# Moving the stored sums of weight blocks from VectorE to GpSimd, with 12 instead of 14 seven-product pairs per half and six load buffers in even turns

## The chip, the core and the metric

The kernel is written in Bass with the Tile scheduler and runs on one core of a Trainium2 chip. The metric is the device time of one launch in microseconds (us), the median of the runs shown. TensorE (PE) multiplies, VectorE (DVE) and ScalarE (ACT) do elementwise work, GpSimd (POOL) does elementwise work and issues DMAs from its own queue, and SyncE (SP) issues most DMAs.

## The reference

One layer of a hybrid block over 256 rows of 2048 channels, in float32:

```python
h = _rmsnorm(x, attn_norm);  proj = h @ w_in            # 2048 x 13,896
# three branches: stick-breaking attention, top-k sparse attention, memory cross-attention
merged = (gates[:, :, 0] * (o_sb @ w_branch[0]) + gates[:, :, 1] * (o_dsa @ w_branch[1])
          + gates[:, :, 2] * (o_mem @ w_branch[2]))
x = x + merged @ w_out
h2 = _rmsnorm(x, ffn_norm)
u = _causal_dwconv(h2 @ w_up, conv_w, conv_b)           # 2048 x 11,008
g, val = jnp.split(u, 2, axis=-1)
return x + (jax.nn.silu(g) * val) @ w_down              # 5504 x 2048
```

Nearly all of the work is streaming weights once through TensorE: 256 rows are two blocks of 128, and every weight is used for both.

## The kernel before, in words

**Weight tiles.** `weight_tiles` lists all weights in the order of use, as tiles of 128 x 1024 float32 (512 KB). For each, `w_tiles` (L165) loads it on SP's queue into one of four `raw` buffers, ACT rounds it to `whi` (L172), DVE subtracts to get the remainder `wlo` (L173), and PE multiplies hi by hi, lo by hi and hi by lo (L104, three matmuls for one product). `whi` and `wlo` have three buffers each. L172 and L173 are issued at high priority: the scheduler, which fixes each engine's order before the run, may put them ahead of work written earlier.

**Stages.** Keys and values of the memory and the projections (weight tiles 1 to 107); then three merges of 48 tiles each, with 48 tiles of stick-breaking projections after the first; then 32 tiles of `w_out`; then 172 tiles of `w_up` with the convolution; then `w_down` in two halves of 1024 columns. In a merge (L577) each of four column chunks takes 8 gate tiles into the PSUM tile `pg`, then DVE adds the bias (L588, `th`), ACT takes tanh (L589), 4 branch tiles go into `pb`, and DVE multiplies and adds (L596, L597, `acc`). In the merge that `turn_merged` follows, PE transposes `acc` (L810) and ACT and DVE split it into `mg` (L205, L209). The stick-breaking projections end each 4-tile chunk with ACT L757 and DVE L758 (`skT`, `sqT`).

**Pairs in w_down.** The 43 blocks of 128 rows of `w_down` go in pairs. A plain pair takes two tiles and 8 block products (24 matmuls, 12 for each tile). A seven-product pair (`Half.seven`, L983) uses sums of blocks instead: 7 products (21 matmuls), but four loads: half a tile, one tile, and two tiles of stored sums. `SEVEN` (L44) lists which pairs of 0 to 21 are made so. The first two loads go to `raw`, the stored sums to `w_t`, two buffers in the pool `dn` (L993).

**Stored sums.** The sums of weight blocks are made earlier in the same launch, as side work: a generator `weight_sums` (L282) that `step` advances once per weight tile. Each unit (a pair and a half) has two 512 KB loads on GpSimd's queue (L290), four DVE subtractions of 128 x 512 (L293) and two 512 KB stores (L312). Two buffers of 1 MB alternate. 17 units run in steps of 8 tiles from the first merge on, 11 more in steps of 6 from the last merge on. The subtractions are issued under `keep_in_program_order`, and so is each L173 while side work is under way, in w_tiles:

```python
low = nc.vector.tensor_sub(lo[:, :kn * n], raw[:, :kn * n], hi[:, :kn * n].bitcast(F32))
if side:
    tc.keep_in_program_order(low)
```

Instructions so marked keep the order in which they are written among themselves.

## Time and profile before

| What | Value |
|---|---|
| Median of 3 runs | 1878.86 us (1871.59 to 1879.55) |
| Profiled execution: its own time / its span | 1879.46 us / 1877.7 us |
| Granted TensorE clock, mean | 0.98 |
| PE / DVE / ACT / POOL busy, share of the span | 92% / 64% / 49% / 4% |
| HBM read / written | 380.85 MB / 35.91 MB |
| Chain that ended last, by engine | PE 53%, DMA 5%, DVE 5%, ACT 4%, issue 3% |

The shares are averages over stages. A view by stretches of time shows how busy each engine was in each stage, the granted clock, and what the DMA engines moved; the view of waits says which instruction an idle engine waited for. [...]

### The profile page before, as it was taken

What the parts mean: (1) busy time and instruction counts of PE and PEld (TensorE: products, weight loads), DVE (VectorE), ACT (ScalarE), POOL (GpSimd) and SP (SyncE); (2) the same over time, 40 slices, a digit from 0 to 9 for tenths busy, and PEclk for the clock granted to TensorE, in tenths of its full rate; (3) what the DMA queues carried; (4) which work ended last, traced back from release to release, by engine and by line L of the source; (5) the groups of instructions that cost most, each with busy time, mean ns of one, the idle gap of its engine ahead of it and who ended that gap; (6) DMA issues with size and microseconds to landing.
All of it is one profiled execution on the core that took longest, in us unless ns stands there. A gap on an engine that the chain in (4) does not pass through costs nothing.

```text
span 1877.7 us, 22959 instructions
## 1 busy us (share of the span) xinstructions
PE 1736.8 (92%) x8334; PEld 1434.0 (76%) x8334; DVE 1208.3 (64%) x1839; ACT 913.9 (49%) x1217; POOL 72.9 (4%) x182
## 2 busy tenths in 40 slices
PE   8999999999878998888888899999999999898988
PEld 6888889777767777676666678888888888566666
DVE  6696665876445556445555557787877787556656
ACT  6555544344336355333333345555555555445453
POOL 0000000000000100000100000000000000000000
PEclk9999999999999999899999999999999999999999
DMA  8855456577665767666777765555556666878885
GB/s 310 281 188 171 155 168 217 179 252 280 231 213 189 262 234 252 207 201 233 252 242 243 267 206 187 188 190 190 190 190 208 199 207 199 283 252 278 274 264 178
DMA packets 123969, 418.28 MB, mean 223 GB/s; under 512 B 13904, under 2 KB 18896, under 8 KB 123856
## 3 DMA queue, kind: packets, MB, share of 16 engines
q1 hardware_dynamic: 106192, 352.84, 56.3%
q0 software_dynamic: 17088, 63.45, 9.4%
q8 instruction: 65, 1.06, 0.2%
q10 hardware_dynamic: 576, 0.53, 0.1%
q14 instruction: 48, 0.39, 0.1%
HBM read 380.85 MB, written 35.91 MB: 222 GB/s over the span
## 4 chain that ended last, share of the span: by engine, by line
PE 53%; DMA 5%; DVE 5%; ACT 4%; issue 3%; DVEq 0%; SPq 0%; ACTq 0%; POOL 0%; POOLq 0%
PE pj L104 47%; DMA w_t<-sums 5%; PE pj L973 4%; DVE wlo L999 2%; ACT whi L998 2%; DVE wlo L173 2%; ACT whi L172 1%; PE s L973 1%; DVE th L596 0%; DMA w_sums<-in_wts 0%; PE s L104 0%; DVE acc L597 0%; ACT L790 0%; DMA sx<-sx 0%; DMA sums<-w_sums 0%
## 5 line engine op out<-in xcount | busy, mean ns | idle before, releaser
L172 ACT ACTIVATE whi<-raw 128x1024 fp32r<-128x1024 f32 (+2 forms) x503 | 531.5, 1057 | 768.4 <-PE pj L104 606.4
L173 DVE TENSOR_TENSOR wlo<-raw,whi 128x1024 fp32r<-128x1024 f32 (+2 forms) x503 | 609.8, 1220 | 280.8 <-ACT whi L172 279.8
L104 PE MATMUL pj<-whi,xc 128*128 128x512 f32 (+2 forms) x1536 | 480.5, 391 | 1.5 <-ACT whi L172 1.0
L104 PE MATMUL pj<-x2c,whi 128*128 128x512 f32 x1376 | 477.5, 391 | 0.0
L104 PE MATMUL pj<-x2c,wlo 128*128 128x256 f32 x1376 | 386.3, 281 | 0.0
L104 PEld LDWEIGHTS pj<-whi,xc 128*128 128x128 f32 x1536 | 290.9, 192 | 58.5 <-ACT whi L172 1.4
L104 PE MATMUL pj<-wlo,xc 128*128 128x512 f32 (+2 forms) x768 | 301.3, 392 | 28.9 <-DVE wlo L173 28.9
L104 PEld LDWEIGHTS pj<-x2c,whi 128*128 128x128 f32 x1376 | 257.5, 187 | 55.8
L104 PEld LDWEIGHTS pj<-x2c,wlo 128*128 128x128 f32 x1376 | 260.7, 189 | 0.0
L104 PEld LDWEIGHTS pj<-wlo,xc 128*128 128x128 f32 x768 | 147.3, 192 | 62.8 <-DVE wlo L173 35.3
L973 PE MATMUL pj<-whi,fc 128*128 128x512 f32 (+1 forms) x420 | 140.9, 392 | 4.9 <-ACT whi L998 4.4
L999 DVE TENSOR_TENSOR wlo<-w_t,whi 128x1024 fp32r<-128x1024 f32 x56 | 68.0, 1225 | 66.7 <-ACT whi L998 66.5
L973 PEld LDWEIGHTS pj<-whi,fc 128*128 128x128 f32 x420 | 79.6, 191 | 24.3 <-ACT whi L998 7.7
L973 PE MATMUL pj<-wlo,fc 128*128 128x512 f32 (+1 forms) x210 | 85.1, 405 | 13.6 <-DVE wlo L999 11.4
L998 ACT ACTIVATE whi<-w_t 128x1024 fp32r<-128x1024 f32 x56 | 58.5, 1057 | 77.5 <-DMA w_t<-sums 43.0
L104 PE MATMUL pj<-xc,whi 128*128 128x512 f32 x256 | 95.9, 414 | 0.0
L104 PE MATMUL pj<-xc,wlo 128*128 128x256 f32 x256 | 76.1, 297 | 15.2 <-DVE wlo L173 15.2
L104 PE MATMUL pj<-whi,mc 128*128 128x512 f32 x256 | 83.4, 404 | 6.9 <-ACT whi L172 6.9
L104 PE MATMUL pj<-whi,mg 128*128 128x512 f32 x256 | 83.9, 406 | 0.0
L293 DVE TENSOR_TENSOR w_sums<-w_sums 128x512 f32<-128x512 f32 x112 | 76.8, 686 | 4.5 <-DMA w_sums<-in_wts 4.4
L999 DVE TENSOR_TENSOR wlo<-raw,whi 128x512 fp32r<-128x512 f32 (+1 forms) x56 | 52.5, 955 | 28.2 <-ACT whi L998 28.2
L104 PE MATMUL pj<-wlo,mg 128*128 128x512 f32 x128 | 52.6, 411 | 13.3 <-DVE wlo L173 13.3
(261 smaller groups left out, 1930.4 us busy)
## 6 DMA issues: line engine op xcount, KB each, us to landing
raw<-in_wts SPq DMA_DIRECT2D x553, 512.0 KB, 4.2
w_sums<-in_wts POOLq DMA_DIRECT2D x56, 512.0 KB, 5.1
sums<-w_sums POOLq DMA_DIRECT2D x56, 512.0 KB, 6.0
w_t<-sums SPq DMA_DIRECT2D x56, 512.0 KB, 4.5
raw<-in_wts SPq DMA_DIRECT2D x30, 256.0 KB, 4.4
th<-in_bg SPq DMA_DIRECT2D x24, 256.0 KB, 5.8
raw<-in_wts SPq DMA_DIRECT2D x5, 492.0 KB, 3.2
sx<-sx_out POOLq DMA_DIRECT2D x6, 384.0 KB, 4.6
```

Of the source, the lines that this page charges most:

```text
L104: nc.tensor.matmul(o, l, r, start=start, stop=stop, skip_group_check=True)
L172: nc.scalar.activation(hi[:, :kn * n], raw[:, :kn * n], AF.Copy)
L173: low = nc.vector.tensor_sub(lo[:, :kn * n], raw[:, :kn * n], hi[:, :kn * n].bitcast(F32))
L293: tc.keep_in_program_order(nc.vector.tensor_sub(d, x_, y_))
L973: keep(nc.tensor.matmul(o, l[a], r[b], start=first and i == 0, stop=stop and i == 2, skip_group_check=True))
L998: keep(nc.scalar.activation(hi, raw, AF.Copy))
L999: keep(nc.vector.tensor_sub(lo, raw, hi.bitcast(F32)))
```

## The change

- The four subtractions of a unit are issued to GpSimd instead of DVE, between the unit's loads and stores in the same queue, all kept in program order. There is one buffer instead of two. A unit begins with a copy of one column of the newest `wlo` tile to a small tile `pace`, on GpSimd. `L173` (L182 in the changed file) is no longer kept in program order.
- `SEVEN` has 12 pairs instead of 14, 24 units in all (16, then 8), each in steps of 8 tiles. The pairs now come in twos with a plain pair between them.
- In the last stage, loads of either kind of pair take `raw`, `raw` and `raw_more` in turn (four and two buffers); `w_t` is gone. The residual is loaded at block 9 instead of 13.

```diff
-SEVEN = (2, 3, 4, 5, 7, 8, 9, 10, 12, 13, 14, 16, 17, 18)
-UNITS = 17
+SEVEN = (2, 3, 5, 6, 8, 9, 11, 12, 14, 15, 17, 18)
+UNITS = 16
...
+    def buffer():
+        turns[0] += 1
+        if more and turns[0] % 3 == 0:
+            return more[0].tile([P, 1024], F32, name="raw_more", bufs=2)
+        return wraw.tile([P, 1024], F32, name="raw")
...
-        raw = wraw.tile([P, 1024], F32, name="raw")
+        raw = buffer()
...
-                low = nc.vector.tensor_sub(lo[:, :kn * n], raw[:, :kn * n], hi[:, :kn * n].bitcast(F32))
-                if side:
-                    tc.keep_in_program_order(low)
+                nc.vector.tensor_sub(lo[:, :kn * n], raw[:, :kn * n], hi[:, :kn * n].bitcast(F32))
+            now[0] = lo
...
     def weight_sums(w, units, every):
...
-            for i in range(2):
-                nc.gpsimd.dma_start(w[n % 2][:, i], wts[down_at[2 * p + i, c0]])
-        def sub(d, x_, y_):
-            tc.keep_in_program_order(nc.vector.tensor_sub(d, x_, y_))
...
+        a, b = w[:, 0], w[:, 1]
+        for c0, p in units:
+            tc.keep_in_program_order(nc.gpsimd.tensor_copy(pace, now[0][:, 0:1].bitcast(F32)))
+            for i in range(2):
+                tc.keep_in_program_order(nc.gpsimd.dma_start(w[:, i], wts[down_at[2 * p + i, c0]]))
+            for d, x_, y_ in ((a[:, h0], a[:, h1], a[:, h0]), (a[:, h1], a[:, h1], b[:, h1]),
+                              (b[:, h1], b[:, h1], a[:, h0]), (b[:, h0], b[:, h0], b[:, h1])):
+                tc.keep_in_program_order(nc.gpsimd.tensor_sub(d, x_, y_))
             for i in range(2):
-                nc.gpsimd.dma_start(sums_d[c0, p][i], w[n % 2][:, i])
-            for _ in range(every - 5):
+                tc.keep_in_program_order(nc.gpsimd.dma_start(sums_d[c0, p][i], w[:, i]))
+            for _ in range(every):
                 yield
...
-        side.append(weight_sums([h8("w_sums").rearrange("p (i c) -> p i c", c=1024) for i in range(2)], units[UNITS:], 6))
+        side.append(weight_sums(h8("w_sums").rearrange("p (i c) -> p i c", c=1024), units[UNITS:], 8))
...
-                    raw = wraw.tile([P, 1024], F32, name="raw") if j < 2 else dn.tile([P, 1024], F32, name="w_t", bufs=2)
-                    raw = raw[:, :n]
+                    raw = buffer()[:, :n]
...
-                    if before is not None and k == 13:
+                    if before is not None and k == 9:
                         e = residual(c0)
```

How the instructions then stand on their engines is shown at three places.

DVE, the last merge, one column chunk, before (`th<-pj,th` waits for the last of the 8 gate tiles, `th<-th,pj` for the last of the 4 branch tiles):

```order
L293 TENSOR_TENSOR w_sums<-w_sums 128x512
L588 TENSOR_TENSOR th<-pj,th 128x1024
L173 TENSOR_TENSOR wlo<-raw,whi 128x1024
L293 TENSOR_TENSOR w_sums<-w_sums 128x512
L173 TENSOR_TENSOR wlo<-raw,whi 128x1024 x3
L293 TENSOR_TENSOR w_sums<-w_sums 128x512
L596 SCALAR_TENSOR_TENSOR th<-th,pj 128x512 x2
L597 TENSOR_TENSOR acc<-acc,th 128x512 x2
L173 TENSOR_TENSOR wlo<-raw,whi 128x1024
```

and in the changed kernel:

```order
L182 TENSOR_TENSOR wlo<-raw,whi 128x1024 x7
L581 TENSOR_TENSOR th<-pj,th 128x1024
L182 TENSOR_TENSOR wlo<-raw,whi 128x1024 x4
L589 SCALAR_TENSOR_TENSOR th<-th,pj 128x512 x2
L182 TENSOR_TENSOR wlo<-raw,whi 128x1024
L590 TENSOR_TENSOR acc<-acc,th 128x512 x2
L182 TENSOR_TENSOR wlo<-raw,whi 128x1024 x7
```

Counted from the start of the program, 115 `wlo` subtractions stand ahead of the first `th<-pj,th` before, and 117 in the changed kernel; the gate tile it waits for is the 115th tile. At each of the 24 waits of this kind in the three merges the count is the number of the tile waited for before, and two more now.

POOL, the first units, in the changed kernel (before, the same queue held only the loads and stores):

```order
L298 COPY pace<-wlo 128x1
L300 DMA w_sums<-in_wts 128x1024 x2
L303 TENSOR_TENSOR w_sums<-w_sums 128x512 x4
L305 DMA sums_2_98<-w_sums 128x1024 x2
L298 COPY pace<-wlo 128x1
```

The next unit's copy now stands behind the whole unit before it.

SP, the first loads after the residual `e` at the start of the last stage, before:

```order
L930 DMA e_12924<-x2d_96 128x1024 x2
L995 DMA w_t_13005<-sums_0_2_97 128x1024
L995 DMA w_t_13011<-sums_0_2_97 128x1024
L995 DMA raw_13038<-in_wts 128x512
L995 DMA raw_13044<-in_wts 128x1024
L995 DMA raw_13083<-in_wts 128x512
L995 DMA w_t_13050<-sums_0_3_98 128x1024
L995 DMA w_t_13056<-sums_0_3_98 128x1024
```

and in the changed kernel:

```order
L924 DMA e_12891<-x2d_97 128x1024 x2
L171 DMA raw_more_12942<-in_wts 128x1024
L988 DMA raw_more_12972<-sums_0_2_98 128x1024
L988 DMA raw_13005<-in_wts 128x512
L988 DMA raw_more_13011<-in_wts 128x1024
L988 DMA raw_13017<-sums_0_3_99 128x1024
L988 DMA raw_13023<-sums_0_3_99 128x1024
```

The load of a plain tile (block 3) now stands behind `e`, and loads follow in the order of use.

## The prediction

> **What bounds the kernel now.** I first read the busy time by stretches, cut where the stages change. Columns: the stretch, its length, then PE, PEld, DVE, ACT and POOL busy (count), granted clock, DMA share, GB/s.

> ```profile
> 0.00:100.00 100.00, 92.62 (x395) 75.10 (x396) 63.45 (x145) 59.25 (x95) 1.88 (x12) 1.00 0.84 289
> 100.00:314.00 214.00, 213.46 (x1054) 181.28 (x1053) 153.85 (x383) 109.85 (x206) 0.62 (x2) 1.00 0.53 172
> 314.00:1131.00 817.00, 720.60 (x3224) 586.00 (x3222) 449.05 (x606) 338.35 (x418) 59.80 (x115) 0.96 0.68 233
> 1131.00:1599.00 468.00, 468.00 (x2703) 413.17 (x2702) 372.35 (x536) 272.43 (x354) 7.46 (x47) 1.00 0.59 194
> 1599.00:1878.00 279.00, 242.08 (x968) 178.49 (x966) 169.65 (x173) 134.03 (x146) 3.18 (x6) 0.97 0.77 256
> ```

> PE is full in the second and fourth stretch: the projections and w_up are bound by TensorE, and the change touches neither. PE idles 96.4 us (817 - 720.6) in the third, where the side work runs, and 36.9 us in the last. What PE waited for in the third stretch (total, times, longest), then the longest in the last:

> ```profile
> PE pj L104 <- DVE wlo L173: 74.6, 39, 4.2
> PE s L104 <- ACT pT L790: 8.2, 4, 2.6
> PE t L810 <- DVE acc L597: 7.0, 4, 1.8
> ...
> PE pj L973 <- DVE wlo L999: 11.4, 18, 0.8
> ```

> So DVE delivers `wlo` late in the third stretch, though it is busy for only 449 of 817 us. The timeline around one such wait, PE and then DVE:

> ```profile
> 901.81 0.39 PE L104 MATMUL pj<-whi,osb 128*128 128x512 f32 x1
> 904.42 0.50 PE L104 MATMUL pj<-wlo,osb 128*128 128x512 f32 x1 [2.22 <-DVE wlo L173]
> ...
> 902.01 1.23 DVE L588 TENSOR_TENSOR th<-pj,th 128x1024 f32<-128x1024 f32 x1 [5.41 <-PE pj L104]
> 903.15 1.22 DVE L173 TENSOR_TENSOR wlo<-raw,whi 128x1024 fp32r<-128x1024 f32 x1
> 904.28 0.69 DVE L293 TENSOR_TENSOR w_sums<-w_sums 128x512 f32<-128x512 f32 x1
> ```

> DVE sat idle for 5.41 us until PE had finished the gate chunk, did `th`, and only then the `wlo` of the next tile, for which PE waited 2.22 us. That is an order, not a load: `wlo` and L293 keep program order together, L293 has no high priority and stays behind `th`, and so every `wlo` written after it stays there too. The same happens in the stick-breaking projections, with L758 in the place of `th`:

> ```profile
> 535.26 0.69 DVE L758 SCALAR_TENSOR_TENSOR skT<-pj,skT 128x512 f32<-128x512 f32 x1 [7.53 <-ACT skT L757]
> 535.87 2.35 DVE L173 TENSOR_TENSOR wlo<-raw,whi 128x1024 fp32r<-128x1024 f32 x2
> ...
> 537.14 0.39 PE L104 MATMUL pj<-xc,wlo 128*128 128x256 f32 x1 [3.15 <-DVE wlo L173]
> ```

> The idle time also goes with a lower clock:

> ```profile
> 314.00:500.00 186.00, 176.42 (x814) 142.85 (x812) 123.67 (x225) 80.64 (x118) 14.67 (x28) 1.00 0.70 242
> 500.00:615.00 115.00, 94.05 (x494) 80.77 (x493) 50.23 (x59) 52.46 (x63) 7.78 (x15) 0.93 0.58 200
> 615.00:790.00 175.00, 160.30 (x696) 130.50 (x696) 93.74 (x107) 83.58 (x98) 14.88 (x28) 0.97 0.71 246
> 790.00:1006.00 216.00, 181.09 (x744) 144.45 (x744) 111.97 (x125) 71.99 (x72) 15.94 (x30) 0.94 0.69 231
> 1006.00:1131.00 125.00, 108.74 (x478) 87.44 (x479) 69.43 (x93) 49.70 (x70) 6.54 (x15) 0.96 0.69 234
> ```

> The missing clock is 0.07 x 115 + 0.03 x 175 + 0.06 x 216 + 0.04 x 125 = 31 us, of which the busy share (720.6/817) makes 27 us of lost PE work. Where PE does not idle the clock reads 1.00.

> In the last stage the chain of waits shows another limit, a ring of load, ACT, DVE, load:

> ```profile
> 1753.40 4.70 DMA w_t<-sums
> ...
> 1758.21 1.07 ACT whi L998
> ...
> 1759.30 1.24 DVE wlo L999
> ...
> 1760.55 5.00 DMA w_t<-sums
> ```

> One `w_t` buffer turns round in 7.15 us (1753.40 to 1760.55). With two buffers and two stored sums to a pair, a seven-product pair takes that long. First matmuls of three such pairs in a row, and an unstalled stretch of plain tiles:

> ```profile
> 1749.72 0.39 PE L973 MATMUL t<-whi,fc 128*128 128x512 f32 x1
> 1754.92 0.39 PE L973 MATMUL t<-whi,fc 128*128 128x512 f32 x1
> 1761.96 0.39 PE L973 MATMUL t<-whi,fc 128*128 128x512 f32 x1
> ...
> 1738.68 11.22 PE pj L973 x48
> ...
> L973 PE MATMUL pj<-whi,fc x420: 280/390/792, 1599.0 to 1873.3; 128*128 128x512 f32 x132, 128*128 128x256 f32 x8
> ```

> Matmuls follow at (11.22 - 0.39)/47 = 0.23 us: 2.76 us for a tile of 12. The first pair of a run, with its sums loaded ahead, takes 5.20 us, the next 7.04, 1.84 more.

> **The change, part by part.** (1) *The order, third stretch.* Two `wlo` now stand ahead of each `th`. When PE finishes a chunk it has two tiles, 5.5 us, and DVE needs 1.23 for `th` and 1.22 for the next `wlo`. I take away the 74.6 us and the 7.0 us for `acc` (its transposes stood one matmul into the next chunk and now stand two tiles in); the other 14.8 us (8.2 of them for `pT`) stay. With 81.6 of 96.4 us of idle time goes its part of the clock, 27 x 0.85 = 23. That is 105 us at most; at least half, 52, if something else is nearly as late. I take 100, leaving 5 for parts 2 and 3.

> (2) *The subtractions.* DVE loses 112 of these:

> ```profile
> L293 DVE TENSOR_TENSOR w_sums<-w_sums x112: 681/685/693, 345.6 to 1085.9; 128x512 f32<-128x512 f32 x112
> ```

> 77 us, worth nothing by themselves, since DVE was not full. GpSimd gains 96. No GpSimd subtraction is in this trace; the nearest rows of that engine (mean ns after the comma):

> ```profile
> L312 POOL DMA_DIRECT2D sums<-w_sums x56 | 29.9, 534 | 419.2 <-DVE w_sums L293 408.5 <-DVE wlo L173 6.7 <-DVE e L447 3.6
> L648 POOL MEMSET nat<- 128x256 f32 x2 | 0.6, 312 | 299.4 <-PE t L609 296.7 <-issue 2.6
> L327 POOL TENSOR_SCALAR_AFFINE_SELECT nat<-nat 128x128 f32<-128x128 f32 x1 | 0.3, 292 | 0.1
> ```

> By the memset 512 columns cost 2 x 312 = 0.62 us, by the select 4 x 292 = 1.17. I take 1.17, since the select reads as well. [...]

> (3) *The queue.* A unit is now serial in GpSimd's queue. Landing times, from the page's DMA issues:

> ```profile
> raw<-in_wts SPq DMA_DIRECT2D x553, 512.0 KB, 4.2
> w_sums<-in_wts POOLq DMA_DIRECT2D x56, 512.0 KB, 5.1
> sums<-w_sums POOLq DMA_DIRECT2D x56, 512.0 KB, 6.0
> ```

> Old stores land 6.0, loads 5.1, four issues 4 x 0.53, subtractions 4 x 1.17: 17.9 us. The next unit is due 8 tiles, 22.1 us, later, so the `pace` copy finds the queue empty. That matters because the copy reads `wlo`: while it waits, one of three `wlo` buffers cannot be rewritten, and DVE and then PE stop behind it. Loads lose their second buffer, at no cost while 17.9 is under 22.1.

> (4) *Last stage.* Four pairs go from seven to eight products, 12 matmuls or 2.8 us of PE, and four times two loads of half a tile and a tile net fall away. Priced by pair: before 28 x 5.20 + 30 x 2.76 = 228 us against 274 measured (1599.0 to 1873.3); of the 46 extra, 20 sevens that follow a seven take 20 x 1.84 = 37, and 9 are start, middle and clock. After: 24 x 5.20 + 38 x 2.76 = 230. Twelve sevens follow a seven; between 0 and 1.84 each, 0 to 22. Six even buffers turning in 7.15 us give a tile every 1.19, four for a pair in 4.8, under 5.20; but four loads are 1.84 MB in 5.20 us, 353 GB/s, and the busiest stretch above moved 289. Two sevens and a plain pair between (4.7 MB in 15.9 us, 297 GB/s) are at that edge, so I take a third, 8. The 9 stay, and 3 are added since block 3's load now waits behind `e`. With the 4.6 us after the last matmul: 255, 24 less than 279; bounds 247 and 269.

> **Sum.** 314 + (817 - 100) + 468 + 255 = 1754, plus 1.5 us by which the profiled execution (1879.46) exceeds the stretches' 1878: 1755. That execution is 0.6 above the median, so nothing is corrected.

> **Rivals.** *Loads late.* A unit adds four 512 KB transfers to eight tiles: 6.3 MB in 22.1 us, 285 GB/s, as much as the first stretch moved with PE at 93%. ACT already waited for loads in the third stretch, so far behind PE's stalls:

> ```profile
> ACT whi L172 <- DMA raw<-in_wts: 39.7, 20, 3.9
> ```

> If all of it reaches PE: 1795. Against it: attention work between tiles lowers the mean to some 250 GB/s. *The last stage stays at 279 us*, bound by what DMA moves and not by its buffers: 1779. Against it: the bytes fall from 67.1 to 64.0 MB (28 x 1.84 + 30 x 0.52, and 24 and 38). *GpSimd and DVE in each other's way:* if each of the 96 subtractions holds up a `wlo` by its 1.17 us and PE pays, 112 us: 1867; half of it, 1811. Against it: a `wlo` is ready 1.06 + 1.22 us after its buffer is free, and PE takes 5.5, so single delays of 1.17 vanish in 3.2 us of slack. [...] *Slower than before: GpSimd becomes the pacemaker.* The units cover 192 of the stretch's 224 tiles, 614 of 717 us, so the gain of 124 us is gone when 24 units take 738, 30.8 us each; with 13.2 us of DMA that is 4.4 us a subtraction, nearly four times my upper row. At 6 us a unit takes 37.2, the stretch 279 more: 2034.

> **Chances.** Forecast (1730 to 1772) 0.50, loads late or the last stage unchanged (to 1800) 0.26, DVE held up (1800 to 1867) 0.11, quicker still 0.07, pacemaker 0.04, no change 0.02. Range 1718 to 1812. A difference under 0.5% is what a measurement here cannot tell from none: faster 0.94, same 0.02, slower 0.04.

> **What would show it.** Right: PE idle under 25 us in the third stretch with the clock at 0.99 or more, waits for `wlo` under 15 us in all; GpSimd subtractions near 1.2 us and the `pace` copy waiting for DVE, not DVE for it; sevens near 5.2 to 6 us in the last stage. Wrong: `wlo` waiting on GpSimd, `wlo` durations well above 1.22 us, ACT waiting on `raw` with PE idle behind it, or sevens still at 7 us.

## The result, and the profile after

The changed kernel takes 1711.06 us (median of 4 runs, 1705.78 to 1715.57) against 1878.82 us before (1871.59 to 1879.55): a ratio of 0.911, 95% interval 0.908 to 0.915. The forecast was 1755 us with a range of 1718 to 1812, so the direction was right and the gain, 168 us, was larger than forecast (124) and than the range allowed for. The profiled execution took 1705.78 us, its span 1704.1 us, the granted clock was 0.997 on average. The four runs lie in two groups 9 us apart, of which the last section tells more; the profiled one is in the quicker.

The same view by stretches as before, of the changed kernel (stretch, length, then PE, PEld, DVE, ACT and POOL busy with counts, clock, DMA share, GB/s):

```profile
0.00:100.00 100.00, 92.41 (x399) 75.10 (x400) 64.52 (x146) 60.24 (x96) 1.89 (x12) 0.98 0.85 293
100.00:314.00 214.00, 213.46 (x1055) 181.25 (x1054) 152.97 (x381) 109.82 (x206) 0.62 (x2) 1.00 0.51 171
314.00:992.00 678.00, 676.40 (x3215) 564.70 (x3214) 434.23 (x493) 335.31 (x418) 220.91 (x219) 1.00 0.78 268
992.00:1460.00 468.00, 468.00 (x2703) 412.68 (x2702) 369.41 (x526) 271.79 (x352) 6.37 (x45) 1.00 0.58 193
1460.00:1704.00 244.00, 230.00 (x981) 179.55 (x979) 163.22 (x165) 129.52 (x138) 2.13 (x4) 0.99 0.80 277
```

The first, second and fourth stretch kept their lengths. The third fell from 817 to 678 us (-139), the last from 279 to 244 (-35). In the third stretch PE's idle time went from 96.4 us to 1.6, and PE's busy time for nearly the same matmuls (x3224 and x3215; the cuts don't fall on the same one) from 720.6 to 676.4. The clock there reads 1.00, against 0.96.

What PE still waits for in the whole run (total, times, longest), where 74.6 us of waits for `wlo` stood before:

```profile
PE pj L104 <- ACT whi L181: 6.8, 2, 5.1
PE pj L967 <- ACT whi L863: 4.7, 1, 4.7
PE pj L967 <- DVE wlo L864: 1.6, 3, 0.8
PE t L728 <- DVE e L440: 1.3, 1, 1.3
PE pj L104 <- DVE wlo L182: 0.8, 1, 0.8
```

And GpSimd's new work: by tile (min/median/max in ns, first and last start), then its group on the page (busy us, mean ns, idle before it), then what the engine waited for:

```profile
L303 POOL TENSOR_TENSOR w_sums<-w_sums x96: 1281/1620/2339, 327.2 to 922.2; 128x512 f32<-128x512 f32 x96
```

```profile
L303 POOL TENSOR_TENSOR w_sums<-w_sums 128x512 f32<-128x512 f32 x96 | 165.2, 1721 | 129.1 <-DMA w_sums<-in_wts 124.7
```

```profile
POOL pace L298 <- DVE wlo L182: 268.7, 24, 58.5
```

A subtraction takes 1.28 to 2.34 us, 1.72 on average. `pace` waits for DVE 268.7 us in all, 58.5 of them in the pause between the two groups of units, so some 9 us a unit. GpSimd has time to spare, and no `wlo` waits for `pace`.

In the last stage, the first matmuls of the seven-product pairs follow like this:

```profile
1532.99 0.39 PE L967 MATMUL t<-whi,fc 128*128 128x512 f32 x1
1543.65 0.39 PE L967 MATMUL t<-whi,fc 128*128 128x512 f32 x1
1548.89 0.39 PE L967 MATMUL t<-whi,fc 128*128 128x512 f32 x1
1559.55 0.39 PE L967 MATMUL t<-whi,fc 128*128 128x512 f32 x1
```

A first seven takes 5.24 us; a second one together with the plain pair behind it 10.66, which leaves about 5.2 for the seven, as a plain pair takes 24 x 0.227 = 5.44. The 7.04 us that a second seven took before is gone entirely.

### The profile page after: what moved, and what is told of

The parts are those of the page before. It is cut to its first block, busy times and chain, and to the rows that moved or that the text cites. A ratio compares the mean times of both kernels' runs of the same rounds, so it can differ in the third digit from the quotient of the medians.

```text
span 1704.1 us, 22824 instructions
## 1 busy us (share of the span) xinstructions
PE 1680.3 (99%) x8346; PEld 1413.3 (83%) x8346; DVE 1184.4 (70%) x1709; ACT 906.7 (53%) x1207; POOL 231.9 (14%) x282
## 3 DMA queue, kind: packets, MB, share of 16 engines
q8 instruction: 65, 1.06, 0.2%
## 4 chain that ended last, share of the span: by engine, by line
PE 93%; DVE 3%; ACT 2%; DMA 1%; issue 1%; SPq 0%; ACTq 0%; DVEq 0%
PE pj L104 80%; PE pj L967 7%; DVE wlo L992 2%; PE s L104 2%; ACT whi L991 1%; PE s L967 1%; PE o L104 1%; PE o L967 1%; DMA raw<-in_wts 1%; DMA raw_more<-in_wts 0%; DVE wlo L864 0%; PE t L602 0%; DVE wlo L182 0%; PE t L830 0%; PE t L803 0%
## 5 line engine op out<-in xcount | busy, mean ns | idle before, releaser
L182 DVE TENSOR_TENSOR wlo<-raw,whi 128x1024 fp32r<-128x1024 f32 (+2 forms) x503 | 647.1, 1287 | 394.8 <-ACT whi L181 381.7
L104 PE MATMUL pj<-whi,xc 128*128 128x512 f32 (+2 forms) x1536 | 481.2, 387 | 0.5 <-DVE xc L215 0.5
L104 PE MATMUL pj<-x2c,whi 128*128 128x512 f32 x1376 | 477.4, 391 | 0.0
L104 PE MATMUL pj<-x2c,wlo 128*128 128x256 f32 x1376 | 385.5, 280 | 0.0
L104 PEld LDWEIGHTS pj<-whi,xc 128*128 128x128 f32 x1536 | 285.3, 188 | 55.3 <-DVE xc L215 1.0
L104 PEld LDWEIGHTS pj<-x2c,whi 128*128 128x128 f32 x1376 | 257.3, 187 | 56.3
L104 PE MATMUL pj<-wlo,xc 128*128 128x512 f32 (+2 forms) x768 | 293.4, 382 | 0.0
L104 PEld LDWEIGHTS pj<-x2c,wlo 128*128 128x128 f32 x1376 | 260.1, 189 | 0.0
L303 POOL TENSOR_TENSOR w_sums<-w_sums 128x512 f32<-128x512 f32 x96 | 165.2, 1721 | 129.1 <-DMA w_sums<-in_wts 124.7
L104 PEld LDWEIGHTS pj<-wlo,xc 128*128 128x128 f32 x768 | 144.6, 188 | 26.1 <-DVE wlo L182 0.3
L967 PE MATMUL pj<-whi,fc 128*128 128x512 f32 (+1 forms) x460 | 151.2, 389 | 5.1 <-ACT whi L863 4.7
L967 PEld LDWEIGHTS pj<-whi,fc 128*128 128x128 f32 x460 | 86.6, 190 | 23.7 <-ACT whi L863 5.4
L967 PE MATMUL pj<-wlo,fc 128*128 128x512 f32 (+1 forms) x230 | 90.8, 395 | 3.2 <-DVE wlo L864 1.6
L992 DVE TENSOR_TENSOR wlo<-raw,whi 128x1024 fp32r<-128x1024 f32 (+1 forms) x64 | 68.6, 1088 | 35.6 <-ACT whi L991 35.2
L104 PE MATMUL pj<-whi,mc 128*128 128x512 f32 x256 | 82.7, 401 | 6.8 <-ACT whi L181 6.8
L104 PE MATMUL pj<-xc,whi 128*128 128x512 f32 x256 | 88.9, 394 | 0.0
L991 ACT ACTIVATE whi<-raw 128x1024 fp32r<-128x1024 f32 (+1 forms) x64 | 59.9, 949 | 43.1 <-PE pj L967 29.0
L104 PE MATMUL pj<-whi,mg 128*128 128x512 f32 x256 | 81.1, 392 | 0.0
L104 PE MATMUL pj<-xc,wlo 128*128 128x256 f32 x256 | 70.9, 277 | 0.0
L104 PEld LDWEIGHTS pj<-whi,mc 128*128 128x128 f32 x256 | 49.3, 193 | 17.7 <-ACT whi L181 7.5
## 6 DMA issues: line engine op xcount, KB each, us to landing
raw<-in_wts SPq DMA_DIRECT2D x537, 512.0 KB, 3.5
w_sums<-in_wts POOLq DMA_DIRECT2D x48, 512.0 KB, 6.1
sums<-w_sums POOLq DMA_DIRECT2D x48, 512.0 KB, 5.5
raw<-sums SPq DMA_DIRECT2D x32, 512.0 KB, 5.1
raw_more<-in_wts SPq DMA_DIRECT2D x20, 512.0 KB, 4.9
raw_more<-sums SPq DMA_DIRECT2D x16, 512.0 KB, 5.5
```

What stands on the lines that cost most here:

```text
L104: nc.tensor.matmul(o, l, r, start=start, stop=stop, skip_group_check=True)
L303: tc.keep_in_program_order(nc.gpsimd.tensor_sub(d, x_, y_))
L967: keep(nc.tensor.matmul(o, l[a], r[b], start=first and i == 0, stop=stop and i == 2, skip_group_check=True))
L991: keep(nc.scalar.activation(hi, raw, AF.Copy))
L992: keep(nc.vector.tensor_sub(lo, raw, hi.bitcast(F32)))
```

## The experiments

Times without an interval come from one execution, beside runs of the kernel before on the same chip.

### One mark alone: the order of the remainders

The kernel before, except that L173 isn't kept in program order. The subtractions stay on DVE; pairs and buffers stay.

```diff
                 low = nc.vector.tensor_sub(lo[:, :kn * n], raw[:, :kn * n], hi[:, :kn * n].bitcast(F32))
-                if side:
-                    tc.keep_in_program_order(low)
```

> The kernel before with one thing undone: L173 is no longer kept in program order while side work runs. The subtractions stay on VectorE, 28 units, old buffers. Theory A (the order alone made the waits): PE waits for wlo in the side-work stretch fall from 75 us to under 10, the stretch from 817 to about 690 us, the time to 1738 to 1765 us. Theory B (VectorE has to be relieved of the subtractions too): at least half of the waits stay, the time is above 1815 us.

Measured: 1736.57 us, ratio 0.924 (0.920 to 0.928), 1.4 us under the range of Theory A. The third stretch, by the same view:

```profile
314.00:992.00 678.00, 676.07 (x3217) 564.96 (x3216) 455.09 (x607) 335.79 (x416) 58.73 (x114) 1.00 0.81 280
```

It is the stretch of the changed kernel within a microsecond (the first matmul of w_up starts at 980.8 and 981.7 us), with DVE at 455 us and the subtractions still on it. The mark alone gives all 139 us there. Moving the subtractions to GpSimd isn't what freed DVE: DVE was late because of the place of its instructions, not because of their number.

### The mark put back

The changed kernel with L182 kept in program order again; the subtractions stay on GpSimd.

```diff
-                nc.vector.tensor_sub(lo[:, :kn * n], raw[:, :kn * n], hi[:, :kn * n].bitcast(F32))
+                low = nc.vector.tensor_sub(lo[:, :kn * n], raw[:, :kn * n], hi[:, :kn * n].bitcast(F32))
+                if side:
+                    tc.keep_in_program_order(low)
```

> The changed kernel with L182 (the wlo subtraction) kept in program order again while side work runs; the sums are still made by GpSimd. Theory A: the waits for wlo come back, 95 to 139 us on top of 1711, so 1800 to 1850 us. Theory B: VectorE has no side work, so the marking hardly matters: under 1730 us.

Measured: 1846.35 us. The stretch up to w_up and PE's waits:

```profile
314.00:1133.00 819.00, 722.10 (x3217) 587.67 (x3216) 417.04 (x495) 336.76 (x416) 216.78 (x219) 0.96 0.64 222
```

```profile
PE pj L104 <- DVE wlo L182: 70.4, 35, 4.2
PE t L805 <- DVE acc L592: 9.0, 4, 2.8
PE s L104 <- ACT pT L785: 7.8, 4, 2.6
```

All three waits are back, with fewer instructions on DVE than before (x495 against x606). So the wait for `pT`, which the prediction let stay, hung on the same mark. It also corrects the mechanism: no subtraction of sums is left on DVE here, so no L293 can hold a `wlo` behind `th`. In this kernel's instruction order 115 `wlo` stand ahead of the first `th`, as before the change, and 117 without the mark. The mark on `wlo` is enough with no side work on DVE. The GpSimd instructions of a unit bear the mark as well; whether `wlo` marked with nothing else marked would do the same was not tried.

### Six even buffers alone

The kernel before with loads taking `raw`, `raw`, `raw_more` in turn (four and two buffers), 14 pairs, nothing else.

```diff
-                    raw = wraw.tile([P, 1024], F32, name="raw") if j < 2 else dn.tile([P, 1024], F32, name="w_t", bufs=2)
-                    raw = raw[:, :n]
+                    raw = buffer()[:, :n]
```

> The kernel before with the six load buffers in even turns, still 14 pairs in runs of four and three, sums on VectorE and kept order as before. Theory C (the turn-round of two w_t buffers was the limit): every seven-product pair takes 5.2 to 5.3 us, the last stage falls from 274 to about 238 us, the time to about 1843 us. Theory D (what DMA can move was the limit, so that the pattern in twos matters): in a run of four the later pairs stay above 5.8 us, the time falls by no more than 20 us, to 1858 or more.

Measured: 1860.07 us. First matmuls of four sevens in a row:

```profile
1775.93 0.39 PE L983 MATMUL t<-whi,fc 128*128 128x512 f32 x1
1781.13 0.39 PE L983 MATMUL t<-whi,fc 128*128 128x512 f32 x1
1786.34 0.39 PE L983 MATMUL t<-whi,fc 128*128 128x512 f32 x1
1791.56 0.39 PE L983 MATMUL t<-whi,fc 128*128 128x512 f32 x1
```

5.20, 5.21, 5.22: not one of them takes the 7.04 us of before. The last stage's matmuls fell from 274 us to 241 (1612.6 to 1853.9). The turn-round of two `w_t` buffers was the limit, not DMA, which moved 316 GB/s here (1775 to 1798 us). Of these 33 us only 18 show in the time, which by itself would have spoken for Theory D: the third stretch was 5 us longer, and w_up took some 9 us more, of which below.

### The pattern alone

The changed kernel with the old buffers: two `raw` and two `w_t` loads for a seven, which stand in twos.

```diff
-                    raw = buffer()[:, :n]
+                    raw = wraw.tile([P, 1024], F32, name="raw") if j < 2 else dn.tile([P, 1024], F32, name="w_t", bufs=2)
+                    raw = raw[:, :n]
```

> The changed kernel with the old load buffers in the last stage (raw for the first two loads of a pair, two w_t buffers for the stored sums); 12 pairs in twos stay. Theory C: the second pair of each two takes 7 us again, 12 x 1.84 = 22 us more, about 1730 us. Theory D: twos with a plain pair between give the two buffers time enough, under 5 us more than 1711.

Measured: 1718.12 us, between what the two theories gave. The last stage took 253.6 us of matmuls against 239.5 in the changed kernel:

```profile
1529.86 0.39 PE L966 MATMUL t<-whi,fc 128*128 128x512 f32 x1
1542.17 0.39 PE L966 MATMUL t<-whi,fc 128*128 128x512 f32 x1
1547.37 0.39 PE L966 MATMUL t<-whi,fc 128*128 128x512 f32 x1
1559.43 0.39 PE L966 MATMUL t<-whi,fc 128*128 128x512 f32 x1
```

Second sevens are slow again: 12.06 and 12.31 us with the plain pair, 10.66 in the changed kernel. Twelve times about 1.7 us is some 20. Eight came back at the start, where the first seven began 12 us into the stage and not 20: with the old buffers block 3's load doesn't stand behind the residual. Buffers, not the pattern, took the 7-us sevens away.

### No subtractions at all

The changed kernel whose units load and store, and subtract nothing.

```diff
-            for d, x_, y_ in ((a[:, h0], a[:, h1], a[:, h0]), (a[:, h1], a[:, h1], b[:, h1]),
-                              (b[:, h1], b[:, h1], a[:, h0]), (b[:, h0], b[:, h0], b[:, h1])):
-                tc.keep_in_program_order(nc.gpsimd.tensor_sub(d, x_, y_))
```

> The changed kernel with GpSimd's four subtractions of each unit left out; loads and stores stay, so the stored blocks are plain weights and the output is not the reference's. Theory E (the subtractions and their collisions with VectorE vanish in slack): within 0.5% of 1711 us, though the wlo subtractions lose the 37 us they had gained. Rival F (the collisions cost time on the path): more than 10 us faster.

Measured: 1708.81 us, ratio 0.910 (0.907 to 0.913), against 0.911 (0.908 to 0.915) with them. So the 165 us of GpSimd's subtractions cost nothing that can be told from noise, and neither does what they do to DVE. That they do something is plain from `wlo`, with the subtractions and then without:

```profile
L182 DVE TENSOR_TENSOR wlo<-raw,whi x503: 499/1225/2358, 5.1 to 1453.1; 128x1024 fp32r<-128x1024 f32 x165, 128x984 fp32r<-128x984 f32 x2, 128x512 fp32r<-128x512 f32 x1
```

```profile
L182 DVE TENSOR_TENSOR wlo<-raw,whi x503: 502/1226/1228, 5.9 to 1451.2; 128x1024 fp32r<-128x1024 f32 x165, 128x984 fp32r<-128x984 f32 x2, 128x512 fp32r<-128x512 f32 x1
```

One place in the changed kernel, GpSimd and then DVE:

```profile
662.57 6.55 POOL L303 TENSOR_TENSOR w_sums<-w_sums 128x512 f32<-128x512 f32 x4 [3.88 <-DMA w_sums<-in_wts]
...
665.19 1.44 DVE L182 TENSOR_TENSOR wlo<-raw,whi 128x1024 fp32r<-128x1024 f32 x1 [2.17 <-ACT whi L181]
667.85 2.36 DVE L182 TENSOR_TENSOR wlo<-raw,whi 128x1024 fp32r<-128x1024 f32 x1 [1.23 <-ACT whi L181]
```

Beside GpSimd's 6.55 us two `wlo` take 1.44 and 2.36 us instead of 1.22, and four subtractions 6.55 instead of 4 x 1.28. Without the subtractions no `wlo` takes more than 1.23 us. The price on the path is none that the two times show.

### GpSimd's work doubled and multiplied by four

The changed kernel with four, then twelve further subtractions in each unit, into a spare tile, in the same queue (the second kernel has 12 for the 4 of the diff).

```diff
+            for _ in range(4):
+                tc.keep_in_program_order(nc.gpsimd.tensor_sub(spare, a[:, h0], b[:, h0]))
```

> The changed kernel with four more subtractions per unit on GpSimd, into a spare tile that nothing reads (8 instead of 4). A unit then keeps GpSimd some 20 us of the 25 us between two pace copies. Theory E: within 0.5% of 1711 us, the pace copies still wait for wlo, wlo in all some 30 us longer. Rival F: 10 us or more slower.

> The changed kernel with twelve more subtractions per unit on GpSimd into a spare tile (16 instead of 4). A unit then takes GpSimd about 39 us (16 x 1.7, loads 5, stores 5.5, issues), more than the 25 us between two pace copies. Theory G (the pacemaker of the prediction: a late pace copy holds a wlo buffer, VectorE and TensorE stop behind it): 24 units at 39 us instead of 192 tiles at 3.0, 355 us more, 1950 to 2130 us. Rival H (GpSimd just falls behind, and is done before the last stage needs the sums): under 1740 us.

Measured: 1747.09 us and 1983.12 us. What `wlo` waited for `pace`, for eight and for sixteen subtractions, and the first and last `pace` of the 8 units of the second group, for four (the changed kernel), eight and sixteen:

```profile
DVE wlo L182 <- POOL pace L299: 72.6, 15, 7.3
```

```profile
DVE wlo L182 <- POOL pace L299: 278.2, 20, 17.3
```

```profile
753.73 0.18 POOL L298 COPY pace<-wlo 128x1 f32<-128x1 f32 x1 [58.50 <-DVE wlo L182]
909.97 0.18 POOL L298 COPY pace<-wlo 128x1 f32<-128x1 f32 x1 [6.97 <-DVE wlo L182]
```

```profile
776.33 0.18 POOL L299 COPY pace<-wlo 128x1 f32<-128x1 f32 x1 [33.89 <-DVE wlo L182]
959.32 0.20 POOL L299 COPY pace<-wlo 128x1 f32<-128x1 f32 x1
```

```profile
928.32 0.18 POOL L299 COPY pace<-wlo 128x1 f32<-128x1 f32 x1 [19.42 <-DVE wlo L182]
1185.66 0.20 POOL L299 COPY pace<-wlo 128x1 f32<-128x1 f32 x1
```

Seven intervals each: 22.3, 26.1 and 36.8 us a unit. In the first pair of rows the copy waits for DVE, that is, for the weights; in the other two the last copy waits for nothing, since the queue itself is late. The pacemaker of the prediction is real, and with sixteen subtractions the kernel is slower than before the change. The expectation that doubling costs nothing failed: a unit then takes 26.1 us where the weights ask for 22.3. What counts is the pace of the kernel that the work is added to, and not the 30.8 us of the break-even with the kernel before.

The eight-subtraction kernel was run a second time:

> The run e6 again (eight subtractions per unit instead of four), for the level of one execution. What e6's trace gives: the queue of GpSimd took 27.8 us a unit ((959.3 - 319.5)/23) where the weight tiles ask for 25.6 ((910.0 - 322.0)/23 in the changed kernel), and wlo waited 72.6 us for the pacemaker. Theory G' (the queue's unit is 18 us plus 1.23 a subtraction, worked out from 27.8 for eight and 37.6 for sixteen, and it holds the kernel from 25.6 on): 1742 to 1757 again, a unit of 27.5 to 28.1 us. Rival L (e6 was a disturbed execution): within 0.5% of 1711.

Measured: 1741.88 us, with 64.5 us of `wlo` waiting for `pace`. The time lies 0.1 us under the expected interval, so 1747 us was no chance execution. The 27.8 us by which that expectation was reckoned is a mean over all 23 intervals and contains the pause between the two groups of units; inside a group it is 26.1.

### Fourteen pairs

The changed kernel with 14 pairs in runs of up to four, 17 + 11 units, the second group in steps of 6 tiles and the second half's residual at block 13, both as before the change.

```diff
-SEVEN = (2, 3, 5, 6, 8, 9, 11, 12, 14, 15, 17, 18)
-UNITS = 16
+SEVEN = (2, 3, 4, 5, 7, 8, 9, 10, 12, 13, 14, 16, 17, 18)
+UNITS = 17
...
-        side.append(weight_sums(h8("w_sums").rearrange("p (i c) -> p i c", c=1024), units[UNITS:], 8))
+        side.append(weight_sums(h8("w_sums").rearrange("p (i c) -> p i c", c=1024), units[UNITS:], 6))
...
-                    if before is not None and k == 9:
+                    if before is not None and k == 13:
```

> The changed kernel with 14 seven-product pairs per half in runs of up to four and 17 units of sums, instead of 12 in pairs and 16 units; six even load buffers and GpSimd stay. Theory C (turn-round of the load buffers was what made the pairs slow, and DMA has room): the four more pairs of both halves each leave out one product of 8, 0.66 us, so the last stage is 2 to 3 us shorter, and the third stretch grows by 8 more subtractions that cost nothing: 1704 to 1713, within 0.5% of the changed kernel's 1711.06. Rival K (runs of four seven-product pairs need more than DMA can bring, since a pair loads 16 blocks of halves in 5.2 us): the stage is 10 to 25 us longer, 1720 to 1736.

Measured: 1715.03 us, ratio 0.913 (0.911 to 0.916). That is inside 0.5% of the changed kernel, 2 us outside the interval that was written, and neither half came as argued. The last stage's matmuls took 240.7 us (1469.0 to 1709.7), no shorter, though no longer either, with 293 GB/s moved (1469 to 1713 us), so DMA isn't the edge. A seven at 5.20 us saves only 0.24 against a plain pair's 5.44. The third stretch grew by 9 us, since the second group's units come every 6 tiles and GpSimd's queue can't follow; `wlo` waited 24.2 us for `pace`. The first and last `pace` of its 11 units:

```profile
753.35 0.19 POOL L298 COPY pace<-wlo 128x1 f32<-128x1 f32 x1 [31.18 <-DVE wlo L182]
938.73 0.20 POOL L298 COPY pace<-wlo 128x1 f32<-128x1 f32 x1
```

Ten intervals of 18.5 us on average: the time that a unit of four subtractions takes when units follow without a pause. The prediction's 17.9 was close, with its subtractions too short.

### The start of the last stage, and a fourth buffer of split tiles

Two further edits of the changed kernel. In the first, `raw_more` comes into use only with pair 2, and the residual of the first half is loaded at block 9, as in the second half, not ahead of everything. In the second, `whi` and `wlo` have four buffers each instead of three. The second was run alone and with the first. (The residual comes later by the first edit, not earlier as the last of the three texts below has it.)

```diff
-        more.append(dn)
...
-        e, before, shares = residual(0), None, iter(())
+        e, before, shares = None, None, iter(())
...
+                if p == 2 and not more:
+                    more.append(dn)
...
-                    if before is not None and k == 9:
+                    if k == 9:
```

```diff
-    whl = ctx.enter_context(tc.tile_pool(name="whl", bufs=3))
+    whl = ctx.enter_context(tc.tile_pool(name="whl", bufs=4))
```

> The changed kernel with raw_more first used for pair 2 (block 3 takes a raw buffer as before) and the residual of the first half loaded at block 9. If the stall at the start of the last stage comes from block 3's load standing behind the residual and in the pool dn, 7 to 8 us go: about 1703 us. If another late load takes its place: no difference from 1711.

> The changed kernel with four buffers of the split weight tiles instead of three and nothing else. Theory H: TensorE's idle time in the last stage falls from 14 us by up to 10, and the time to 1701 to 1706. Rival I: the stage still takes 244 us, within 3 us, and the time is between 1705 and 1716 as the changed kernel's own runs.

> The changed kernel with two further edits: the residual load of the last stage's first half is put three blocks earlier and its third load stream is first used for pair 2 (the edit of the run e8), and the split weight tiles have four buffers instead of three. Theory H: once the loads of the last stage arrive in time, what stops TensorE there is the hand-over of split tiles: of 244 us it works 230 (after, 1460 to 1704), e8 took about 8 of the 14, and a fourth buffer lets ScalarE and VectorE be one tile further ahead. It takes off up to 24 blocks x 0.42 us = 10 us more: 1688 to 1694, 4 to 10 under e8's 1698. Rival I: there is nothing left to gain there, since TensorE waits for whi and wlo at the start only; within 0.3% of e8's 1698 (1693 to 1703). Rival J: a fourth buffer moves the order of the third stretch too and wlo waits come back: over 1706.

Measured: the start 1698.11 us, ratio 0.903 (0.901 to 0.905); the fourth buffer 1695.27 us; both 1686.98 us, ratio 0.898 (0.896 to 0.900). Median against median, both together beat the changed kernel by 24 us; against its profiled execution, whose w_up ran at the same rate, by 19. Each time lies under what was expected for it: 5 us for the start, 6 for the fourth buffer, 1 for both. In the first the medians mix the two rates of w_up; its last stage's matmuls took 231.7 us against 239.5. Which of its two changes brings this was not separated. What stalled at the start is this wait of the changed kernel, for block 3, and the load at its root (from the chain of that stretch):

```profile
1474.49 0.79 PE L967 MATMUL pj<-whi,fc 128*128 128x512 f32 x1 [4.71 <-ACT whi L863]
```

```profile
1466.17 7.10 DMA raw_more<-in_wts
```

The last stretch with both edits, and three sevens of it:

```profile
1460.00:1687.00 227.00, 221.08 (x985) 181.36 (x983) 163.18 (x164) 128.85 (x138) 2.13 (x4) 1.00 0.84 296
```

```profile
1519.61 0.39 PE L966 MATMUL t<-whi,fc 128*128 128x512 f32 x1
1524.37 0.39 PE L966 MATMUL t<-whi,fc 128*128 128x512 f32 x1
1534.57 0.39 PE L966 MATMUL t<-whi,fc 128*128 128x512 f32 x1
```

A seven now takes 4.76 us, which is 21 matmuls of 0.227; the plain pair keeps its 5.44. The 5.20 us that passed for an unstalled seven in the prediction held 0.44 us that a fourth buffer takes away. Twenty-four times that is 10.6 us, and the fourth buffer alone shortened the last stage's matmuls from 239.5 to 228.7. Its time is 16 us under the changed kernel's median, but 10.5 under that kernel's profiled execution (1705.78), the gain of Theory H.

## Where the prediction was wrong, and what of it was right

**The bound: right.** DVE delivered `wlo` late in the third stretch by its order, and the idle time went with a lower clock. Taking the mark away, and nothing else, left 1.9 us of idle time in the third stretch, at a clock of 1.00.

**Part 1, the size: wrong, and this is the step that failed.** The term "105 us at most", taken as 100, measured 139. Of the 50 us by which the profiled execution is quicker than the sum of 1754, 39 stand here and 11 in the last stage. Two things were too small in the term.

The first is the 14.8 us of idle time (8.2 for `pT` among it) that the prediction let stay, without a reason. They went too: 96.4 us fell to 1.6. The experiment with the mark put back has the waits for `pT` and `acc` again, so they belong to the same cause. For `pT`, PE's own order shows how, in the kernel before and then in the changed one:

```profile
579.55 0.77 PE L104 MATMUL s<-ac,tri 128*128 128x384 f32 x4
582.88 0.49 PE L104 MATMUL s<-sqT,skT 128*128 128x256 f32 x1 [2.56 <-ACT pT L790]
...
621.47 0.69 PE L104 MATMUL s<-ac,tri 128*128 128x384 f32 x4
627.52 0.81 PE L104 MATMUL s<-sqT,skT 128*128 128x256 f32 x4
```

Before, no weight matmul stands between these two steps of the attention, and PE waits for ACT. In the changed kernel 24 weight matmuls stand between them, and PE does these while ACT works. The kernel with only the mark taken away has the same 24 there; the one with the mark put back has none again (584.3 to 587.6 us). The prediction looked at DVE's order, and at PE's for the transposes of `acc` alone; the mark on a DVE instruction had changed PE's order in the attention too.

The second is the price of the clock. The prediction took the missing clock, 31 us, times PE's busy share and times 0.85, 23 us in all. Measured is what PE's busy time fell by for nearly the same matmuls, 44.2 us. The missing clock is indeed 31 us before and nothing after, so the slow clock can bear at most that part. But it falls on matmuls and not evenly on the stretch: it comes just after the waits, when PE is busy again, as in these two rows of the kernel before (two waits of 1.75 and 1.08 us lie in the first):

```profile
1006.47:1009.89 3.42, 1.61 (x8) 1.24 (x9) 3.42 (x6) 0.60 (x1) 0.11 (x1) 1.00 0.24 58
1009.89:1013.30 3.41, 3.41 (x10) 2.63 (x9) 3.41 (x5) 0.04 (x1) 0.42 (x1) 0.50 0.82 243
```

In the slow spells of the third stretch PE was busy for 97% of the time, so that nearly all of the 31 us was PE's loss, and all of it went. Of the other 13 us some 9 are the recorded tail of the last matmul ahead of each wait, which lasts 0.39 us where matmuls follow each other at 0.23 and counts as busy (56 waits x 0.16); that is reckoned, not shown by a run, and the last 4 us are open. What would have served here is the time of the stretch's matmuls alone. The rate at which they run where PE is full can be read in the same trace, with no sum of waits at all: the matmuls of the kernel before from 314 us to the start of w_up, each at the median spacing of its size (0.227 us for 512 columns), make 656 us. The kernel before took 806 for them, the changed one 668.

**Its mechanism: right in what it did, wrong in one link.** That L293 drags `wlo` behind `th` was argued; the experiment shows that the mark on `wlo` does it with no L293 on DVE, and that without the mark L293 on DVE does no harm.

**Part 2, the subtractions: right on the path, too short in themselves.** 1.17 us was taken; 1.72 was measured on average, and 1.28 at the least. Nothing hung on it.

**Part 3, the queue: right.** 17.9 us a unit was forecast, 18.5 measured where units follow without a pause, and `pace` waits for DVE. That the two are so close is partly luck: in those ten units four subtractions took 6.5 us on average, 1.8 more than priced, and the rest of a unit 12.0 instead of 13.2.

**Part 4, the last stage: 255 forecast, 244 measured.** The 8 us for second sevens at the edge of DMA were 0: the edge, at 289 GB/s, was the author's estimate, and the changed kernel moved 307 from 1532 to 1560 us. The run with fourteen pairs has no such edge either. The start cost what was feared, 8 us by the run that removes it (239.5 to 231.7), against 9 + 3 for start, middle and clock together.

**The rivals.** Loads late: no; in the third stretch ACT waited for `raw` once, for 0.8 us, and PE idled for 1.6 us in all. The last stage unchanged: no. GpSimd and DVE in each other's way: that a subtraction holds up a `wlo` by its whole 1.17 us was an assumption that no row of the kernel before shows. In the changed kernel a `wlo` of 1.22 us takes up to 2.36, and the time is the same without subtractions; that the 3.2 us of slack named in the prediction is what covers it fits, but was not tried. The pacemaker: not at four subtractions; it was made at sixteen. The prediction set its break-even with the kernel before at 30.8 us a unit; between 26.1 us (a span of 1745.4) and 36.8 (1981.4) the straight line crosses the span before, 1877.7, at 32.1.

**The range** stopped at 1718 because no case carried a third stretch shorter than the sum of named waits. "Quicker still" had a chance of 0.07 and no working of its own.

## What to carry to other kernels

Price a stretch whose stalls go away from below, by its matmuls at the rate of a full stretch, and use the sum of waits only to see which edit reaches it: waits that look separate can hang on one order. A mark that keeps instructions in program order can cost lookahead on the engine that bears it, though that engine is half idle (here DVE was busy for 417 of 819 us), and can reorder another engine's work: compare the order on every engine before pricing. When side work is moved to a queue of its own, compare a unit of it with the pace of the new kernel, not of the old.

## What the runs showed of the hardware that was not expected

```profile
L104 PE MATMUL pj<-x2c,whi 128*128 128x512 f32 x1376 | 477.4, 391 | 0.0
```

```profile
L104 PE MATMUL pj<-x2c,whi 128*128 128x512 f32 x1376 | 486.4, 399 | 0.0
```

The clock is 1.00 and PE full in both, and the second takes 9 us more. The runs of the changed kernel lie in two groups 9 us apart (1705.78 and 1707.53, 1714.59 and 1715.57), as do those with the other start (four from 1696.2 to 1698.45, two of 1705.04 and 1707.75). That these groups are w_up's two rates is inferred: one trace of each kernel was kept. The profile names no cause, and none was tried.
- GpSimd's subtraction of 128 x 512 takes 1.28 us at the least and up to 2.34 us beside DVE's `wlo`, which itself goes from 1.22 to as much as 2.36 us. The one that begins later bears the wait in the changed kernel's trace. All 49 `wlo` (L182) that take over 1.3 us began while a subtraction was running, and those that began while none was take 1.23 us at most; the 21 subtractions that began while DVE was idle take 1.28 to 1.30. In the place shown above the fourth subtraction begins 0.01 us ahead of the second `wlo` and takes 1.29 us, and that `wlo` takes 2.36.
